# A projection kernel's first loads: single row tiles of x between the first k-tiles of w, cast and turned one row at a time, with fewer dummy matmuls

## The chip, the cores and the metric

One core of one Trainium2 chip. The metric is device time in microseconds (us) of one execution, as the median of several runs. A profile of one execution covers a span some 1.8 us shorter than the time of the same run.

## The reference

```python
def reference(x, w_qkv):              # x [16, 512, 768] f32, w_qkv [768, 2304] f32
    qkv = np.matmul(x, w_qkv)
    q, k, v = qkv[..., :768], qkv[..., 768:1536], qkv[..., 1536:]
    return np.stack([q, k, v], axis=0).astype(np.float32)
```

It is one product of 8192 x 768 by 768 x 2304, written out as three pieces.

## The kernel before

The x rows are handled in 32 pairs of row tiles (2 x 128 rows). From the fourth pair on, each pair is multiplied by a scheme that saves products, with sums of blocks of x made by GpSimd and sums of blocks of w made by VectorE. The first three pairs are multiplied plainly while those sums are being made. The change touches only the start of this plain part. "Turning" is a transpose on TensorE into PSUM, copied out by VectorE (first half) and ScalarE (second half). `busy(n)` issues n dummy 128x512 matmuls of zeros, to keep TensorE active until there is work.

```python
def load_rows(p):                      # two row tiles, 768 KB in one load
    xin[p] = xin_pool.tile([P, 2, K], fp32, name="xin")
    rows = x_flat[p * 2 * P:(p + 1) * 2 * P, :]
    nc.sync.dma_start(xin[p][:], rows.rearrange("(r m) k -> m r k", m=P))
...
load_rows(0)
...
load_rows(1)
load_blocks(0, 0, 1)                   # first w block: six k-tiles of 256 KB
load_w(st_rem[:], 0, KT, R_OFF, REM)   # 256 remainder columns of w
load_rows(2)
load_blocks(0, 1)                      # second w block, 768 KB halves
...
singles = [((0, ), (0, 1)), ((1, ), (0, 1)), ((0, 1), (2, 3))]     # (k-tiles, row tiles)
singles += [((j, ), range(4)) for j in range(2, KT)]
...
busy(11)
cast_rows(0)
turn_rows(0)
busy(4)
cast_rows(1)
cast_k(0)
cast_k(1)
turn_rows(1)
for j in range(2, KT):
    cast_k(j)
... # cast of the remainder columns
block(0, 0, b1[0], singles, nothing)   # four row tiles, first w block
rem(0)
rem(1)                                 # the same rows, remainder columns
cast_rows(2, False)
turn_rows(2, False)
block(0, 0, b1[0], halves((4, 5)), nothing)
... # second w block: the marker of this study
```

Of the kernel before, what the change touches and what calls it, by code (L numbers as in the profile page):

```python
# [10 lines left out]
def kernel(  # L11
# [20 lines left out]
    nc = tc.nc  # L32
    P = 128
# [3 lines left out]
    K = H  # L37
    N3 = w_qkv.shape[1]
    KT = K // P
    KH = KT // 2  # L40
    KC = K // 4
    NP = M // (2 * P)
    CB = 512
    REM = N3 - 4 * CB
    Q_OFF = (0, 2 * CB + REM)
    R_OFF = 2 * CB
    fp32 = mybir.dt.float32
    f32r = mybir.dt.float32r
    bf16 = mybir.dt.bfloat16
    ident = mybir.ActivationFunctionType.Identity  # L50
# [3 lines left out]
    x_flat = x.rearrange("b t h -> (b t) h")  # L54
# [5 lines left out]
    tq_pool = ctx.enter_context(tc.tile_pool(name="tq", bufs=2))  # L60
# [4 lines left out]
    xin_pool = ctx.enter_context(tc.tile_pool(name="xin", bufs=3))  # L65
    xf_pool = ctx.enter_context(tc.tile_pool(name="xf", bufs=2))
    xb_pool = ctx.enter_context(tc.tile_pool(name="xb", bufs=4))
    s_pool = ctx.enter_context(tc.tile_pool(name="s", bufs=2))
    ps_pool = ctx.enter_context(tc.tile_pool(name="ps", bufs=8, space=bass.MemoryType.PSUM))

    w_rem = w_pool.tile([P, KT, REM], bf16, name="w_rem")

    b1 = [w_pool.tile([P, KT, CB], bf16, name=f"b1_{q}") for q in range(2)]
# [7 lines left out]
    def load_w(dst, j0, nj, off, cols):  # L81
        rows = w_qkv.rearrange("(p j) n -> p j n", j=KT)
        nc.sync.dma_start(dst, rows[:, j0:j0 + nj, off:off + cols])

    stage = {}

    def load_blocks(q, c, nj=KH):
        if q == 0:
            t = tq_pool.tile([P, KT, CB], fp32, name="st0", tag="tq")
            for j in range(0, KT, nj):  # L90
                load_w(t[:, j:j + nj], j, nj, Q_OFF[q] + c * CB, CB)
            stage[q, 0, c], stage[q, 1, c] = t[:, :KH, :], t[:, KH:, :]
        else:
            for h in range(2):
                t = st_pool.tile([P, KH, CB], fp32, name="st1", tag="st")
                load_w(t[:], h * KH, KH, Q_OFF[q] + c * CB, CB)
                stage[q, h, c] = t[:]
# [11 lines left out]
    xin, xf, xb, sr = {}, {}, {}, {}  # L109
# [19 lines left out]



    def load_rows(p):
        xin[p] = xin_pool.tile([P, 2, K], fp32, name="xin")
        rows = x_flat[p * 2 * P:(p + 1) * 2 * P, :]
        nc.sync.dma_start(xin[p][:], rows.rearrange("(r m) k -> m r k", m=P))

    def copy_halves(dst, src, two):

        nc.vector.tensor_copy(out=dst[0], in_=src[0])  # L139
        if two:  # L140
            nc.scalar.activation(dst[1], src[1], ident)  # L141
        else:
            nc.vector.tensor_copy(out=dst[1], in_=src[1])

    xc = {}

    def cast_rows(p, two=True):
        src = xin.pop(p)
        xc[p] = s_pool.tile([P, 2, K], bf16, name="xc", tag="s")
        for r in range(2):  # L150
            halves = (slice(0, K // 2), slice(K // 2, K))
            copy_halves([xc[p][:, r, n] for n in halves], [src[:, r, n] for n in halves], two)

    def turn_rows(p, two=True):
        c = xc.pop(p)
        xb[p] = xb_pool.tile([P, KT, 2 * P], bf16, name="xb")
        for r in range(2):
            cols = c[:, r, :].rearrange("m (p j) -> m j p", j=KT)
            ps = ps_pool.tile([P, KT, P], bf16, name="ps")
            for j in range(KT):  # L160
                nc.tensor.transpose(ps[:, j, :], cols[:, j, :], eye)  # L161
            ks = (slice(0, KH), slice(KH, KT))
            copy_halves(
                [xb[p][:, n, r * P:(r + 1) * P] for n in ks], [ps[:, n, :] for n in ks], two
            )

    def round_x(p):
        xb[p] = xb_pool.tile([P, KT, 2 * P], bf16, name="xb")
# [42 lines left out]
    def bank():  # L211
        return ps_pool.tile([P, CB], fp32, name="ps")
# [29 lines left out]
    def rows_of(s, p, lo, hi):  # L242
        return out_flat[s, p * 2 * P:(p + 1) * 2 * P, lo:hi].rearrange("(r m) n -> m r n", m=P)

    def store_quad(u):
        if u.q == 0:
            nc.sync.dma_start(rows_of(0, u.p, 0, H), u.o[:, :, :H])
            nc.sync.dma_start(rows_of(1, u.p, 0, 2 * CB - H), u.o[:, :, H:])
        else:
            part = 2 * H - Q_OFF[1]  # L250
            nc.sync.dma_start(rows_of(1, u.p, H - part, H), u.o[:, :, :part])
            nc.sync.dma_start(rows_of(2, u.p, 0, H), u.o[:, :, part:])

    def rem_row(p, r, ps):
        for j in range(KT):
            nc.tensor.matmul(  # L256
                ps, xb[p][:, j, r * P:(r + 1) * P], w_rem[:, j, :],
                start=(j == 0), stop=(j == KT - 1), skip_group_check=True,
            )

    def rem(p):
        ps = ps_pool.tile([P, 2, REM], fp32, name="ps")
        for r in range(2):
            rem_row(p, r, ps[:, r, :])
        o = or_pool.tile([P, 2, REM], fp32, name="orem")
        nc.scalar.activation(o[:], ps[:], ident)  # L266
        nc.sync.dma_start(rows_of(1, p, R_OFF - H, R_OFF - H + REM), o[:])
# [70 lines left out]
    NS = 3  # L338
    zero = w_pool.tile([P, CB], bf16, name="zero")
    nc.vector.memset(zero[:], 0.0)  # L340
    load_rows(0)
    tiny = w_pool.tile([P, 1], fp32, name="tiny")
    nc.scalar.activation(tiny[:], zero[:, :1], ident)

    eye = w_pool.tile([P, 240], bf16, name="eye")[:, :P]
    make_identity(nc, eye)
    load_rows(1)
    load_blocks(0, 0, 1)
    st_rem = o_pool.tile([P, KT, REM], fp32, name="str", tag="o")
    load_w(st_rem[:], 0, KT, R_OFF, REM)  # L350
    load_rows(2)
    load_blocks(0, 1)
    load_blocks(1, 0)
    load_blocks(1, 1)
    load_x(3, nc.sync)
# [2 lines left out]
    def busy(n):  # L358

        ps = bank()  # L360
        for _ in range(n):
            nc.tensor.matmul(ps[:], zero[:, :P], zero[:], start=True, stop=True)  # L362
# [9 lines left out]
    def block(q, c, w, groups, cast_next):  # L372


        ps = {}
        for js, tiles in groups:
            for n in tiles:
                p, r = divmod(n, 2)
                if n not in ps:
                    ps[n] = bank()  # L380
                for j in js:
                    nc.tensor.matmul(  # L382
                        ps[n][:], xb[p][:, j, r * P:(r + 1) * P], w[:, j, :],
                        start=(j == 0), stop=(j == KT - 1), skip_group_check=True,
                    )
                if KT - 1 not in js:
                    continue
                if r == 0:
                    cast_next(p)
                u = quads[q][p]  # L390
                nc.scalar.activation(u.o[:, r, c * CB:(c + 1) * CB], ps[n][:], ident)
                if c == 1 and r == 1:
                    store_quad(u)

    def halves(tiles):
        return [(range(h * KH, (h + 1) * KH), tiles) for h in range(2)]


    singles = [((0, ), (0, 1)), ((1, ), (0, 1)), ((0, 1), (2, 3))]
    singles += [((j, ), range(4)) for j in range(2, KT)]  # L400

    act, dve = nc.scalar, nc.vector
    def cast_k(j):
        dve.tensor_copy(out=b1[0][:, j, :], in_=stage[0, j // KH, 0][:, j % KH, :])

    def cast_next(q, c, w):
        return lambda p: p < 2 and cast(q, p, c, w, act)

# [1 line left out]
        dve.tensor_copy(out=b1[0][:, j, :], in_=stage[0, j // KH, 0][:, j % KH, :])  # L410

    nothing = lambda p: None
    busy(11)
    cast_rows(0)
    turn_rows(0)
    busy(4)
    cast_rows(1)
    cast_k(0)
    cast_k(1)
    turn_rows(1)  # L420
    for j in range(2, KT):
        cast_k(j)
    act.activation(w_rem[:, KH:], st_rem[:, KH:], ident)
    dve.tensor_copy(out=w_rem[:, :KH], in_=st_rem[:, :KH])
    bt0 = bt_pool.tile([P, KT, CB], bf16, name="bt")
    bt1 = bt_pool.tile([P, KT, CB], bf16, name="bt")

    block(0, 0, b1[0], singles, nothing)
    rem(0)
    rem(1)  # L430
    cast_rows(2, False)
    turn_rows(2, False)
    block(0, 0, b1[0], halves((4, 5)), nothing)
    for h in range(2):
        cast(0, h, 1, bt0, dve)
    for n in range(1, 5):
        sum_w(0, n)
    dve.tensor_copy(out=b22[0][:], in_=stage[0, 1, 1])
    block(0, 1, bt0, halves(range(6)), cast_next(1, 0, b1[1]))
    load_x(4, nc.sync)  # L440
    block(1, 0, b1[1], halves(range(6)), cast_next(1, 1, bt1))
# [56 lines left out]
```

## Time and profile before

| | kernel before |
|---|---|
| time, median of the first three runs | 362.76 us (362.67 to 362.77) |
| span of the profiled run (which took 363.17 us) | 361.4 us |
| TensorE (PE) busy | 353.3 us, 98% |
| dummy matmuls | 15 |
| second w block starts at | 20.54 us |

The prediction below shows the lines. A timeline line reads: start, length, engine, line of the kernel, operation, tiles, count, and in brackets how long the engine was idle before and what released it. Merged matmul lines include the drain of the last one, so a length is a little over count times pace.

### The profile page before, as it was taken

Reading aid. Unit: us, or ns where it says so; the run is one execution under the profiler, and the core shown is the slowest. Engines: PE = TensorE matmul, PEld = TensorE weight load, DVE = VectorE, ACT = ScalarE, POOL = GpSimd, SP = SyncE. Lnnn points to the kernel's source line nnn. Section 1 sums busy time; section 2 is a strip of 40 time slices with the busy share of each in tenths; the row PEclk is TensorE's granted clock in tenths of the full one; section 3 lists DMA queues with packets and bytes.
Section 4 is the critical chain, followed back from the end, with each engine's and each line's share of the span. In section 5 each row is a group of like instructions: output and inputs, shape, how many; then the busy total and the mean of one; then the engine's idle time right before and its main releaser. Section 6 shows DMA issues by size and latency. Waiting matters only on the chain.

```text
span 361.4 us, 5220 instructions
## 1 busy us (share of the span) xinstructions
PE 353.3 (98%) x1765; PEld 250.8 (69%) x1797; DVE 222.7 (62%) x239; ACT 182.5 (51%) x304; POOL 174.4 (48%) x180
## 2 busy tenths in 40 slices
PE   8999999999999999999999999999999999999994
PEld 3644577777777777777777777777777777777763
DVE  3489546666566765566675565676556676556642
ACT  4547555455454545454545444445545454545452
POOL 0000970566664445664445665444666444566410
PEclk9999999999999999999999999999999999999999
DMA  7999969799899989999999999898999998989766
GB/s 294 381 383 338 348 227 345 271 354 304 279 322 298 296 275 296 282 313 314 284 278 295 282 306 316 284 276 291 295 285 317 295 296 276 297 279 331 267 251 242
DMA packets 80617, 108.08 MB, mean 299 GB/s; under 512 B 4816, under 2 KB 60368, under 8 KB 80592
## 3 DMA queue, kind: packets, MB, share of 16 engines
q1 hardware_dynamic: 65184, 96.35, 82.3%
q10 hardware_dynamic: 15408, 11.41, 9.9%
q8 instruction: 14, 0.23, 0.3%
q14 instruction: 11, 0.09, 0.1%
HBM read 32.24 MB, written 75.50 MB: 298 GB/s over the span
## 4 chain that ended last, share of the span: by engine, by line
PE 96%; ACT 1%; issue 1%; ACTq 0%; DVE 0%
PE ps L206 75%; PE ps L256 11%; PE ps L382 9%; PE ps L362 1%; PE ps L161 1%; ACT o L237 0%; ACTq L297 0%; ACT xb L141 0%; ACT orem L311 0%; DVE xb L139 0%; ACT xc L141 0%; ACTq L313 0%; DVE zero L340 0%; ACTq L311 0%
## 5 line engine op out<-in xcount | busy, mean ns | idle before, releaser
L206 PE MATMUL ps<-t,s 128*128 128x512 f32 x696 | 173.8, 398 | 0.0
L206 PEld LDWEIGHTS ps<-t,s 128*128 128x128 f32 x696 | 130.7, 188 | 29.8
L169 POOL CAST xb<-xf 128x1536 bf16<-128x1536 f32 x29 | 46.4, 1601 | 167.7 <-DVE xf L124 167.7
L234 DVE TENSOR_TENSOR o<-o,ps 128x512 f32<-128x512 f32 x58 | 39.9, 688 | 87.6 <-ACT o L233 87.6
L124 DVE STREAM_TRANSPOSE xf<-xin 128x1536 f32<-128x1536 f32 x29 | 85.7, 2956 | 9.7 <-DMA xin<-in_x_dram 7.1
L206 PE MATMUL ps<-b,xb 128*128 128x512 bf16 x320 | 82.4, 380 | 1.5
L233 ACT ACTIVATE o<-ps 128x512 f32<-128x512 f32 x58 | 34.7, 598 | 44.3 <-PE ps L206 44.3
L206 PEld LDWEIGHTS <-xb 128*128 128x128 bf16 x348 | 31.7, 98 | 35.6 <-issue 7.6
L227 ACT ACTIVATE o<-ps 128x512 f32<-128x512 f32 x58 | 34.8, 600 | 40.0 <-PE ps L206 37.3
L240 DVE TENSOR_TENSOR o<-o,ps 128x512 f32<-128x512 f32 x58 | 39.9, 688 | 21.4 <-PE ps L206 20.2
L206 PE MATMUL ps<-b,s 128*128 128x512 f32 x174 | 48.7, 389 | 0.0
L256 PE MATMUL ps<-w_rem,xb 128*128 128x256 bf16 x384 | 47.2, 273 | 0.0
L237 ACT ACTIVATE o<-ps 128x512 f32<-128x512 f32 x58 | 34.7, 598 | 24.1 <-PE ps L206 21.3
L220 ACT ACTIVATE o<-ps 128x512 f32<-128x512 f32 x58 | 34.6, 597 | 23.8 <-DVE o L240 20.7
L256 PEld LDWEIGHTS <-xb 128*128 128x128 bf16 x384 | 37.4, 98 | 11.2 <-issue 0.5
L224 DVE TENSOR_TENSOR o<-o,ps 128x512 f32<-128x512 f32 x58 | 36.5, 673 | 3.4 <-PE ps L206 2.1
L206 PEld LDWEIGHTS ps<-b,s 128*128 128x128 f32 x174 | 32.7, 188 | 6.8
L178 POOL TENSOR_TENSOR s<-s,xf 128x384 fp32r<-128x384 f32 x29 | 29.5, 1016 | 2.3
L266 ACT ACTIVATE orem<-ps 128x512 f32<-128x512 f32 x31 | 18.6, 598 | 22.7 <-PE ps L256 21.4
L179 POOL TENSOR_TENSOR s<-xf 128x384 fp32r<-128x384 f32 x29 | 29.5, 1017 | 0.0
L181 POOL TENSOR_TENSOR s<-xf,s 128x384 fp32r<-128x384 f32 x29 | 29.4, 1015 | 0.0
L177 POOL TENSOR_TENSOR s<-xf 128x384 fp32r<-128x384 f32 x29 | 29.3, 1012 | 0.0
(36 smaller groups left out, 127.2 us busy)
## 6 DMA issues: line engine op xcount, KB each, us to landing
out_dram<-o SPq DMA_DIRECT2D x62, 768.0 KB, 5.1
out_dram<-o SPq DMA_DIRECT2D x65, 256.0 KB, 4.6
xin<-in_x_dram SPq DMA_DIRECT2D x62, 192.0 KB, 6.7
xin<-in_x_dram ACTq DMA_DIRECT2D x54, 192.0 KB, 4.5
out_dram<-orem SPq DMA_DIRECT2D x31, 256.0 KB, 5.5
st<-in_w_qkv_dram SPq DMA_DIRECT2D x6, 768.0 KB, 14.1
xin<-in_x_dram SPq DMA_DIRECT2D x3, 768.0 KB, 5.8
st<-in_w_qkv_dram SPq DMA_DIRECT2D x6, 256.0 KB, 6.3
```

The costliest lines, as they stand in the source:

```text
L124: nc.vector.transpose(t[:].rearrange("p j (g b) -> p g j b", b=G), xin.pop(p)[:].rearrange("p g (a j) -> p g j a", a=G),)
L169: nc.gpsimd.tensor_copy(out=xb[p][:], in_=xf[p][:])
L206: nc.tensor.matmul(ps[:], lhs[j], rhs[j], start=(start and j == 0), stop=(j == KH - 1), skip_group_check=True,)
L220: nc.scalar.activation(c11, u.x[:], ident)
L224: nc.vector.tensor_tensor(c11, c11, u.z[:], op=add)
L227: nc.scalar.activation(c12, u.x[:], ident)
L233: nc.scalar.activation(c22, u.x[:], ident)
L234: nc.vector.tensor_tensor(c22, c22, u.y[:], op=add)
L237: nc.scalar.activation(c21, u.x[:], ident)
L240: nc.vector.tensor_tensor(c12, c12, u.y[:], op=add)
L256: nc.tensor.matmul(ps, xb[p][:, j, r * P:(r + 1) * P], w_rem[:, j, :], start=(j == 0), stop=(j == KT - 1), skip_group_check=True,)
L382: nc.tensor.matmul(ps[n][:], xb[p][:, j, r * P:(r + 1) * P], w[:, j, :], start=(j == 0), stop=(j == KT - 1), skip_group_check=True,)
```

## The change

The intent: the first row tile is usable one transfer sooner if it is not tied to the second, and a fourth row tile is not needed until the first three have been multiplied by five k-tiles. So rows 0, 1 and 2 come singly, then k-tiles 0 to 4, row 3, k-tile 5; casts and turns are done row by row, and fewer dummies should be needed. The remainder's two halves, of which ScalarE cast one before, are both cast by VectorE.

```diff
-    load_rows(0)
+    load_row(0, 0)                     # 384 KB each
 ...
-    load_rows(1)
-    load_blocks(0, 0, 1)
+    load_row(0, 1)
+    load_row(1, 0)
+    for j in range(KT - 1):
+        load_k(j)
+    load_row(1, 1)
+    load_k(KT - 1)
-    load_w(st_rem[:], 0, KT, R_OFF, REM)
-    load_rows(2)
+    for h in range(2):
+        load_w(st_rem[:, h * KH:(h + 1) * KH], h * KH, KH, R_OFF, REM)
+    for r in range(2):
+        load_row(2, r)
 ...
-    busy(11)
-    cast_rows(0)
-    turn_rows(0)
-    busy(4)
-    cast_rows(1)
-    cast_k(0)
-    cast_k(1)
-    turn_rows(1)
-    for j in range(2, KT):
+    busy(8)
+    cast_row(0, 0)
+    cast_row(0, 1)
+    turn_row(0, 0)
+    busy(1)
+    cast_row(1, 0)
+    turn_row(0, 1)
+    cast_k(0)
+    turn_row(1, 0)
+    for j in range(1, KT - 1):
         cast_k(j)
 ... (helpers by row; the fourth row's cast and turn stand between k-tiles 4 and 5)
-    block(0, 0, b1[0], singles, nothing)
-    rem(0)
-    rem(1)
-    cast_rows(2, False)
-    turn_rows(2, False)
-    block(0, 0, b1[0], halves((4, 5)), nothing)
+    block(0, 0, b1[0],
+        [((j, ), range(3)) for j in range(KT - 1)]
+        + [fourth_row, ((KT - 1, ), range(3)), (range(KT), (3, ))], nothing)
+    for p in range(2):
+        rem(p)
+        cast_row(2, p, False)
+        turn_row(2, p, False)
+    block(0, 0, b1[0], [(range(KT), (4, )), (range(KT), (5, ))], nothing)
```

More of the change, by code (lines that the diff above doesn't have):

```diff
@@ L128, in transpose, with load_row @@
         xf[p] = t
-    def load_rows(p):
-        xin[p] = xin_pool.tile([P, 2, K], fp32, name="xin")
-        rows = x_flat[p * 2 * P:(p + 1) * 2 * P, :]
-        nc.sync.dma_start(xin[p][:], rows.rearrange("(r m) k -> m r k", m=P))
+    def load_row(p, r):
+        if r == 0:
+            xin[p] = xin_pool.tile([P, 2, K], fp32, name="xin")
+        row = (2 * p + r) * P
+        nc.sync.dma_start(xin[p][:, r, :], x_flat[row:row + P, :])
     def copy_halves(dst, src, two):
@@ L145, with cast_row, turn_row @@
     xc = {}
-    def cast_rows(p, two=True):
-        src = xin.pop(p)
-        xc[p] = s_pool.tile([P, 2, K], bf16, name="xc", tag="s")
-        for r in range(2):
-            halves = (slice(0, K // 2), slice(K // 2, K))
-            copy_halves([xc[p][:, r, n] for n in halves], [src[:, r, n] for n in halves], two)
-    def turn_rows(p, two=True):
-        c = xc.pop(p)
-        xb[p] = xb_pool.tile([P, KT, 2 * P], bf16, name="xb")
-        for r in range(2):
-            cols = c[:, r, :].rearrange("m (p j) -> m j p", j=KT)
-            ps = ps_pool.tile([P, KT, P], bf16, name="ps")
-            for j in range(KT):
-                nc.tensor.transpose(ps[:, j, :], cols[:, j, :], eye)
-            ks = (slice(0, KH), slice(KH, KT))
-            copy_halves(
-                [xb[p][:, n, r * P:(r + 1) * P] for n in ks], [ps[:, n, :] for n in ks], two
-            )
+    def cast_row(p, r, two=True):
+        if r == 0:
+            xc[p] = s_pool.tile([P, 2, K], bf16, name="xc", tag="s")
+        halves = (slice(0, K // 2), slice(K // 2, K))
+        copy_halves([xc[p][:, r, n] for n in halves], [xin[p][:, r, n] for n in halves], two)
+    def turn_row(p, r, two=True):
+        if r == 0:
+            xb[p] = xb_pool.tile([P, KT, 2 * P], bf16, name="xb")
+        cols = xc[p][:, r, :].rearrange("m (p j) -> m j p", j=KT)
+        ps = ps_pool.tile([P, KT, P], bf16, name="ps")
+        for j in range(KT):
+            nc.tensor.transpose(ps[:, j, :], cols[:, j, :], eye)
+        ks = (slice(0, KH), slice(KH, KT))
+        copy_halves(
+            [xb[p][:, n, r * P:(r + 1) * P] for n in ks], [ps[:, n, :] for n in ks], two
+        )
     def round_x(p):
@@ L346, with load_k @@
     make_identity(nc, eye)
-    load_rows(1)
-    load_blocks(0, 0, 1)
-    st_rem = o_pool.tile([P, KT, REM], fp32, name="str", tag="o")
-    load_w(st_rem[:], 0, KT, R_OFF, REM)
-    load_rows(2)
-    load_blocks(0, 1)
+    st_0 = tq_pool.tile([P, KT, CB], fp32, name="st0", tag="tq")
+    stage[0, 0, 0], stage[0, 1, 0] = st_0[:, :KH, :], st_0[:, KH:, :]
+    def load_k(j):
+        load_w(st_0[:, j:j + 1], j, 1, Q_OFF[0], CB)
+    load_row(0, 1)
[4 more added lines that the diff above has]
+    load_k(KT - 1)
+    st_rem = o_pool.tile([P, KT, REM], fp32, name="str", tag="o")
+    for h in range(2):
+        load_w(st_rem[:, h * KH:(h + 1) * KH], h * KH, KH, R_OFF, REM)
+    for r in range(2):
+        load_row(2, r)
+    load_blocks(0, 1, KH)
     load_blocks(1, 0)
@@ L375, in block @@
         ps = {}
-        for js, tiles in groups:
+        for group in groups:
+            if callable(group):
+                group()
+                continue
+            js, tiles = group
             for n in tiles:
@@ L396, in halves @@
         return [(range(h * KH, (h + 1) * KH), tiles) for h in range(2)]
-    singles = [((0, ), (0, 1)), ((1, ), (0, 1)), ((0, 1), (2, 3))]
-    singles += [((j, ), range(4)) for j in range(2, KT)]
     act, dve = nc.scalar, nc.vector
-    def cast_k(j):
-        dve.tensor_copy(out=b1[0][:, j, :], in_=stage[0, j // KH, 0][:, j % KH, :])
     def cast_next(q, c, w):
@@ L412, with fourth_row @@
     nothing = lambda p: None
-    busy(11)
-    cast_rows(0)
-    turn_rows(0)
-    busy(4)
-    cast_rows(1)
+    busy(8)
[5 more added lines that the diff above has]
+    turn_row(0, 1)
     cast_k(0)
-    cast_k(1)
-    turn_rows(1)
-    for j in range(2, KT):
+    turn_row(1, 0)
+    for j in range(1, KT - 1):
         cast_k(j)
-    act.activation(w_rem[:, KH:], st_rem[:, KH:], ident)
-    dve.tensor_copy(out=w_rem[:, :KH], in_=st_rem[:, :KH])
+    def fourth_row():
+        cast_row(1, 1)
+        cast_k(KT - 1)
+        turn_row(1, 1)
+        for h in range(2):
+            ks = slice(h * KH, (h + 1) * KH)
+            dve.tensor_copy(out=w_rem[:, ks], in_=st_rem[:, ks])
     bt0 = bt_pool.tile([P, KT, CB], bf16, name="bt")
     bt1 = bt_pool.tile([P, KT, CB], bf16, name="bt")
-    block(0, 0, b1[0], singles, nothing)
-    rem(0)
-    rem(1)
-    cast_rows(2, False)
-    turn_rows(2, False)
-    block(0, 0, b1[0], halves((4, 5)), nothing)
+    block(
+        0, 0, b1[0],
+        [((j, ), range(3)) for j in range(KT - 1)]
+        + [fourth_row, ((KT - 1, ), range(3)), (range(KT), (3, ))],
+        nothing,
+    )
+    for p in range(2):
[3 more added lines that the diff above has]
+    block(0, 0, b1[0], [(range(KT), (4, )), (range(KT), (5, ))], nothing)
     for h in range(2):
```

## The prediction

> **What bounds the kernel now.** I read the page first: busy shares, then the chain that ended last. Then I asked for PE's waits over the whole run, and for the first 22 us in order of time, because the change touches nothing later.
>
> ```profile
> PE 353.3 (98%) x1765; PEld 250.8 (69%) x1797; DVE 222.7 (62%) x239; ACT 182.5 (51%) x304; POOL 174.4 (48%) x180
> ...
> PE 96%; ACT 1%; issue 1%; ACTq 0%; DVE 0%
> PE ps L206 75%; PE ps L256 11%; PE ps L382 9%; PE ps L362 1%; PE ps L161 1%; ACT o L237 0%; ACTq L297 0%; ACT xb L141 0%; ACT orem L311 0%; DVE xb L139 0%; ACT xc L141 0%; ACTq L313 0%; DVE zero L340 0%; ACTq L311 0%
> ```
>
> PE is the chain almost everywhere. Line 362 is the group of dummy matmuls that bridges the wait for the first rows; it is on the chain but computes nothing. PE's waits, all of them in the run:
>
> ```profile
> PE ps L362 <- DVE zero L340: 1.2, 1, 1.2
> PE ps L161 <- ACT xc L141: 0.6, 1, 0.6
> ```
>
> Both are before 8.5 us. After that PE waits for nothing the profile resolves, so what counts is how early PE can start useful work and never stop. The start in order of time (start, length, engine, line):
>
> ```profile
> 0.74 0.95 SPq L135 DMA_DIRECT2D xin<-in_x_dram  x2
> 1.19 4.88 PE L362 MATMUL ps<-zero 128*128 128x512 bf16 x11 [1.19 <-DVE zero L340]
> 5.08 0.94 ACT L141 ACTIVATE xc<-xin 128x384 bf16<-128x384 f32 x2 [2.85 <-DMA xin<-in_x_dram]
> 5.86 1.11 PE L161 MATMUL ps<-eye,xc 128*128 128x128 bf16 x12
> 6.81 1.03 PE L362 MATMUL ps<-zero 128*128 128x512 bf16 x4
> 7.07 0.87 ACT L141 ACTIVATE xb<-ps 128x384 bf16<-128x384 bf16 x2 [1.05 <-DVE xb L139]
> 8.40 0.95 PE L161 MATMUL ps<-eye,xc 128*128 128x128 bf16 x12 [0.57 <-ACT xc L141]
> 9.19 5.34 PE L382 MATMUL ps<-b,xb 128*128 128x512 bf16 x23
> 11.11 0.43 DVE L410 CAST b<-st 128x512 bf16<-128x512 f32 x1 [0.26 <-DMA st<-in_w_qkv_dram]
> 13.37 0.56 DVE L424 CAST w_rem<-str 128x768 bf16<-128x768 f32 x1 [1.83 <-DMA str<-in_w_qkv_dram]
> 14.37 2.78 PE L256 MATMUL ps<-w_rem,xb 128*128 128x256 bf16 x24
> 15.43 0.36 DVE L139 CAST xc<-xin 128x384 bf16<-128x384 f32 x1 [1.50 <-DMA xin<-in_x_dram]
> 16.99 0.83 PE L161 MATMUL ps<-eye,xc 128*128 128x128 bf16 x12
> 17.94 2.76 PE L382 MATMUL ps<-b,xb 128*128 128x512 bf16 x11
> 20.54 7.93 PE L382 MATMUL ps<-bt,xb 128*128 128x512 bf16 x36
> ```
>
> The reader should see three things. The first 768 KB of x are usable at 5.08 us, and PE fills the time with dummies. From 6.97 to 8.40 PE again does nothing useful: four dummies and a gap, until the second pair of rows is loaded and cast. From 8.40 to 20.54 PE is full: 12 transposes, 24 matmuls, 24 remainder matmuls, 12 transposes, 12 matmuls. I take 20.54, where the second w block starts, as the marker: everything after it is the same program in both kernels.
>
> **What the Trainium skill says.** "TensorE: Matmul & The Clock Gate", section "What's actually happening": the array runs at half clock until about 3.4 us of sustained activity have been seen. The trace agrees: the dummies start 0.43 us apart, the real 128x512 matmuls run at 0.216 (24 from 9.19 to 14.37). The granted-clock row of the page does not show it (9 tenths in every slice). "DMA: Bandwidth & Descriptors", section "Latency and other measured facts", speaks of a fixed cost of about 2 us for a DMA. Here the first load is issued at 0.74 and usable at 5.08, 4.34 us; its 786 thousand bytes at the measured 400 GB/s take 1.97, so 2.4 us are fixed, which agrees. "PSUM — Partial Sum Buffer", section "PSUM bank collisions raise a hardware error", says that two engines must not touch one bank at once. The trace agrees in form: ACT's copy out of the transposed bank (7.07) starts only when DVE's 0.36 us copy of it, from 6.67, is over.
>
> **The change part by part.**
>
> Loads. Bytes are the same, the order is not: x row tiles 0, 1, 2 (393 thousand bytes each, 0.98 us at 400 GB/s), k-tiles 0 to 4 of w (262 thousand, 0.66 us each), row tile 3, k-tile 5, the remainder block in two halves, rows 4 and 5. The stream starts at 0.74 + 2.4 = 3.1 us in landing times. Rows land at about 4.1, 5.1 and 6.1; k-tiles at 6.7, 7.4, 8.0, 8.6, 9.3; row 3 at 10.3; k-tile 5 at 11.1 as before (same bytes ahead of it; DVE had waited for it at 11.11). The remainder's halves land at 12.3 and 13.37, rows 4 and 5 at 14.4 and 15.43, the later ones again as before. Five more issues at about 0.45 us of SP's queue each cost nothing: the built program lets eight loads be outstanding, and at any time these hold over 2 MB, 5 us of stream.
>
> Dummies. 11 + 4 become 8 + 1. Eight at 0.43 us end at 1.19 + 3.42 = 4.61; the first row's casts end at 4.1 + 0.52 (ACT's half) = 4.6. So useful work starts at 4.65 instead of 5.86, 1.2 us earlier.
>
> From there I walk PE, each start being the later of PE free and data ready. Durations are from the rows above and from single instructions of the same groups: DVE cast 0.35, ACT cast 0.52, DVE copy out 0.36, ACT copy out 0.45, k-tile cast 0.43, six transposes 0.64 cold and 0.4 warm.
> Row 0 turned 4.65 to 5.3, dummy to 5.6, row 1 turned 5.6 to 6.1. Row 2 is cast by 6.65 (ACT, after its copy for row 0), but its turn ends about 7.1. k-tile 0 is cast at 7.14 (DVE: two other steps first).
> Blocks of 3 matmuls, 0.65 each: k0 7.15 to 7.8, k1 8.0 to 8.65, k2 to 9.3, k3 to 9.95, k4 to 10.6. Row 3 (landed 10.3, cast by 10.8) turns 10.85 to 11.25. k5 is cast 11.1 to 11.53: 11.55 to 12.2. Tile 3 by itself, 6 matmuls: 12.2 to 13.5.
> Remainder: three matmuls of 0.109 to 13.83, then a wait for the second half (13.37 + 0.56 = 13.93), nine more to 14.95.
> Row 4 is cast 14.4 to 15.03, turned 15.1 to 15.5; remainder of rows 2 and 3 15.5 to 16.8; row 5 cast by 16.85, turned to 17.3. Two tiles of 6 matmuls (1.3 each): 17.3 to 19.9.
> The second block starts at 19.9 instead of 20.54: 0.64 us earlier.
>
> So of the 1.2 us at the start and the 1.43 at 6.97, some 2 us come back as small gaps: DMA pace between k-tiles, row 3, the remainder's second half. A check from the other side: the second half of the remainder cannot be used before 13.95, and 21 remainder matmuls (2.29), 12 transposes (0.8) and 12 matmuls (2.6) follow it, 5.7 us, so 19.65 is the floor while the loads keep their times.
>
> What follows must not eat the gain. The second block's first half is cast by DVE from about 18.0 (its copies end there), 0.95, done 18.9: before 19.9. Its second half is usable at 20.87 + 0.96 = 21.83; PE needs it 18 matmuls (3.9) after 19.9, at 23.8. The next block's first half is cast by ACT until 24.3, needed at 27.7. The POOL sums for the first group of Strassen-like products end at 45.8, needed at 48.2 (48.88 less the gain). Each has 2 us or more of room. At the end PE is again the chain up to 353 us, so the shift reaches the end. Predicted: 362.76 - 0.64 = 362.1.
>
> **The rivals.**
> First, cold clock. The dummies now stop sooner and small gaps stand among transposes from 5.3 to 7.1, so the gate may open late. For: in the kernel before it opened near 6.6 after unbroken work. Against: the share of work in that window is still about nine tenths. If it stays cold to 9.9, the block up to there does 6 matmuls instead of 12 and PE is about 1.2 us late at 10.6; part of that fits in the waits after it, and the marker comes at about 20.2. Time 362.4; with a longer cold stretch 363.
> Second, the loads set the end and the gain is nothing. For: the remainder's cast was at 13.37 and its use at 14.37, close behind; the DMA share is full in this window. If the smaller loads land some 0.5 us later than their bytes say, the remainder and rows 4, 5 push PE back to where it was: 362.6 to 362.8.
> Third, more gain. The gaps I count for row 5 and the remainder may be hidden, or DMA may begin with the small row sooner than I think; the floor of 19.65 gives 361.9, and if remainder halves land earlier than the whole did, 361.5.
> Fourth, the earlier stores and loads of the next stage collide. DMA engines are full from 16 to 40 us, but PE needs nothing from them sooner than 2 us after their old landings, so I give it little.
>
> **Range and chances.** The centre is the walk, 362.1. The cold clock and late loads bound it above, the floor with a little more below: 361.6 to 362.7 for 8 in 10. Two per cent are 7.3 us; all time before useful work is 5.9 us, plus 1.4 later, so a faster verdict is out of reach, and a slower one would need the start to double. Faster 0.005, within 2% 0.99, slower 0.005.
>
> **What would show it.** First transposes near 4.65 (step one), first real matmul near 7.15, k-tile groups spaced 0.65 by the casts, remainder from 13.5, second block near 19.9, and the steady stage shifted by the same amount with its 10.7 us period unchanged. The prediction is wrong if matmuls of the first block take 0.43 us, if the first row is not usable before 4.6, or if PE shows waits after 20 us that the kernel before did not have.

## More of the kernel before

One view is added here, because the answer turned on it. It has one line for a stretch of time: the stretch, its length, busy time of PE, PEld (weight loads), DVE (VectorE), ACT (ScalarE) and POOL (GpSimd), the granted share of the TensorE clock, the busy share of the DMA engines, and GB/s. Kernel before, 4 to 6 us:

```profile
4.00:6.00 2.00, 2.00 (x7) 0.72 (x6) 0.63 (x2) 0.92 (x2) 0.00 (x0) 1.00 1.02 412
```

The loads stream at 412 GB/s here.

## The result and the profile after

Measured: 364.21 us median of six runs (363.08 to 364.34), against 362.74 of the kernel before (six runs, 362.67 to 363.44). The ratio is 1.0031, with a 95% interval of 1.0017 to 1.0046. Ratios here are the mean time of one kernel's runs over that of the other's of the same rounds, so not quite the ratio of the medians. The forecast was 0.7 us faster; it came out about 1.1 to 1.5 us slower. By the 2% rule both are "same", but the sign is clear.

PE's waits in the changed kernel (total, times, longest), all of them:

```profile
PE ps L160 <- ACT xc L142: 1.6, 2, 1.4
PE ps L374 <- DVE zero L339: 1.2, 1, 1.2
```

The wait for a cast row (line 160 is the turn) grew from 0.6 to 1.6 us. The start in order of time:

```profile
0.74 1.34 SPq L136 DMA_DIRECT2D xin<-in_x_dram  x3
1.18 3.52 PE L374 MATMUL ps<-zero 128*128 128x512 bf16 x8 [1.18 <-DVE zero L339]
3.75 0.52 ACT L142 ACTIVATE xc<-xin 128x384 bf16<-128x384 f32 x1 [1.53 <-DMA xin<-in_x_dram]
4.54 0.50 PE L160 MATMUL ps<-eye,xc 128*128 128x128 bf16 x6
4.87 0.52 ACT L142 ACTIVATE xc<-xin 128x384 bf16<-128x384 f32 x1 [0.60 <-DMA xin<-in_x_dram]
...
5.45 0.54 PE L160 MATMUL ps<-eye,xc 128*128 128x128 bf16 x6 [0.20 <-ACT xc L142]
...
6.81 0.52 ACT L142 ACTIVATE xc<-xin 128x384 bf16<-128x384 f32 x1 [0.78 <-DMA xin<-in_x_dram]
7.39 0.54 PE L160 MATMUL ps<-eye,xc 128*128 128x128 bf16 x6 [1.40 <-ACT xc L142]
7.99 5.03 PE L399 MATMUL ps<-b,xb 128*128 128x512 bf16 x15
11.82 0.43 DVE L420 CAST b<-st 128x512 bf16<-128x512 f32 x1 [0.34 <-DMA st<-in_w_qkv_dram]
12.86 0.50 PE L160 MATMUL ps<-eye,xc 128*128 128x128 bf16 x6
21.16 7.93 PE L399 MATMUL ps<-bt,xb 128*128 128x512 bf16 x36
```

The first two rows are early: usable at 3.75 and 4.87, both before the 5.08 of the pair. The third row comes at 6.81, not at 6.1. Then 15 matmuls take 5.03 us, where the walk had 3.45 us (7.15 to 10.6). The second block starts at 21.16 instead of 20.54. From there on the two kernels take the same: 23.31 us each for the three other plain blocks, and for the rest 317.4 us (changed) and 317.6 us (before). All of the profiled difference arises before 21 us. The two profiled runs took 363.17 us (before) and 363.70 us (changed), so this pair of traces shows only 0.5 us of the difference.

Two things show in the view by stretches, for the changed kernel:

```profile
4.00:6.00 2.00, 1.79 (x15) 0.89 (x13) 0.74 (x3) 1.26 (x3) 0.00 (x0) 1.00 0.97 320
```

```profile
4.51:7.91 3.40, 1.81 (x20) 1.19 (x19) 1.65 (x5) 1.98 (x4) 0.00 (x0) 1.00 0.96 336
7.93:11.32 3.39, 3.33 (x8) 1.13 (x8) 2.18 (x7) 0.72 (x3) 0.00 (x0) 0.50 1.05 393
11.34:14.74 3.40, 3.40 (x22) 1.70 (x21) 1.86 (x5) 1.26 (x4) 0.00 (x0) 1.00 1.07 382
```

First, the loads fell from 412 to 320 GB/s between 4 and 6 us, although the DMA engines count as busy. Second, the granted clock was 0.50 from 7.92 to 11.33. In the 3.4 us just before, PE had been busy for 1.81. The trace's own clock records, which no line here shows, give the edges as 4.506 (full), 7.919 (half), 11.332 (full): 3.413 us apart each time. The time in front of the first record counts as full clock in this view, though the dummies there ran 0.43 us apart; so the page's clock row does not show a late opening.

Two causes were thus on the table. "Clock": with fewer dummies and a longer pause, the clock gate (closed, TensorE runs at half clock) closes again or opens late. "Loads": small loads at the start make the stream itself slower.

### The profile page after: what moved, and what is told of

Read it like the earlier page. It is cut to its first block, busy times and chain, and to the rows that moved or that the text cites. A ratio compares the mean times of both kernels' runs of the same rounds, so it can differ in the third digit from the quotient of the medians.

```text
span 361.9 us, 5243 instructions
## 1 busy us (share of the span) xinstructions
PE 354.7 (98%) x1791; PEld 250.1 (69%) x1791; DVE 225.5 (62%) x240; ACT 182.3 (50%) x303; POOL 173.8 (48%) x180
## 4 chain that ended last, share of the span: by engine, by line
PE 96%; DMA 1%; ACT 1%; ACTq 0%; SPq 0%; issue 0%; DVE 0%
PE ps L205 75%; PE ps L255 11%; PE ps L399 9%; DMA st<-in_w_qkv_dram 1%; SPq L136 0%; ACT o L236 0%; ACTq L296 0%; PE ps L160 0%; ACT orem L310 0%; DVE b L420 0%; ACTq L312 0%; ACTq L310 0%
## 5 line engine op out<-in xcount | busy, mean ns | idle before, releaser
L168 POOL CAST xb<-xf 128x1536 bf16<-128x1536 f32 x29 | 43.8, 1512 | 168.9 <-DVE xf L124 134.5
L205 PE MATMUL ps<-b,xb 128*128 128x512 bf16 x348 | 84.9, 380 | 0.0
L176 POOL TENSOR_TENSOR s<-xf 128x384 fp32r<-128x384 f32 x29 | 30.8, 1064 | 0.0
L178 POOL TENSOR_TENSOR s<-xf 128x384 fp32r<-128x384 f32 x29 | 29.5, 1016 | 0.0
```

Of the source, the lines that this page charges most:

```text
L168: nc.gpsimd.tensor_copy(out=xb[p][:], in_=xf[p][:])
L205: nc.tensor.matmul(ps[:], lhs[j], rhs[j], start=(start and j == 0), stop=(j == KH - 1), skip_group_check=True,)
```

## The experiments

Kernels of one call ran on the same chip, each call on another one, and shared the runs of the kernel before: 362.77 us median in the first call (11 runs), 362.99 in the second (9), 362.83 in the third (11). Its runs are not all alike either: they fall near 362.7 and near 363.3, so a tenth of a per cent needs the intervals. All results were correct.

### again: the changed kernel once more

No edit.

> The changed kernel unaltered, for more runs and a second trace. Theory clock (the gate closes again in the gap before the third row's turn): times scatter between about 363.0 and 364.4, and a trace with a long time has a stretch at half clock after 4.5 us or opens late. Theory loads (the small first loads land late): the third row tile again lands near 6.8 us instead of 6.1, in every trace alike, and the times do not scatter.

Measured: 363.70 us (362.97 to 364.69, 6 runs), ratio 1.0024 (1.0010 to 1.0038). The times scatter by 1.7 us, as theory clock says, though the loads differ between the two traces too. The second trace shows the gate closing too, in another place:

```profile
3.93:7.33 3.40, 1.61 (x15) 0.82 (x13) 0.83 (x4) 1.38 (x4) 0.00 (x0) 1.00 0.85 288
7.35:10.75 3.40, 2.95 (x12) 1.48 (x13) 2.53 (x8) 1.38 (x3) 0.00 (x0) 0.50 1.04 404
```

Half clock from 7.34 to 10.75, again 3.41 us, after a stretch of the same length in which PE was busy for 1.61. The third row was cast at 7.22 us, later still; so theory loads holds in both traces of this kernel, but not its claim that times would not scatter.

The record also holds the mean granted clock of every run. A half-clock stretch of 3.41 us takes 0.005 off it, and no trace without such a stretch after the opening is below 0.997. Nine of the changed kernel's twelve runs have 0.992 to 0.995, so the gate very probably closed in each of them. The two fastest, 363.08 and 362.97 us, have 1.000. One of 364.20 us has 0.999; why it was slow is not shown.

### fill5: dummies into the gap

```diff
     turn_row(0, 1)
+    busy(5)
     cast_k(0)
```

> The changed kernel with five dummy matmuls more, between the second row's turn and the third row's, where PE waited 1.4 us. Theory clock: no half-clock stretch after opening, the first block's matmuls at 0.22 us, spread under 0.5 us, time about 362.2 to 362.8, so 1.4 us or more faster than the changed kernel. Theory loads: the third row still comes at 6.8 us, and the time stays at 363.5 or more.

Measured: 363.20 us (362.91 to 363.64, 5 runs), ratio 1.0009 (0.9997 to 1.0021), 0.5 us under the unaltered kernel.

```profile
3.40:6.80 3.40, 3.40 (x18) 1.82 (x17) 1.29 (x5) 1.85 (x4) 0.00 (x0) 1.00 0.93 303
6.81:10.20 3.39, 3.37 (x20) 1.54 (x19) 2.25 (x7) 1.18 (x3) 0.00 (x0) 1.00 1.04 392
```

The gate opened at 6.81 and stayed open; the first block's 15 matmuls took 3.70 us instead of 5.03, and the spread fell to 0.7 us. All five runs have a mean clock of 0.997 or more. That is theory clock. But the loads still ran at 303 GB/s in the first of these stretches, the third row was cast at 6.49, and the second block began at 20.68. The gain was a third of what theory clock alone had promised, and neither theory's time was met. The trace shows both causes at work. The difference of the times alone is less sure, as the intervals of the two kernels overlap (1.0009, 0.9997 to 1.0021, against 1.0024, 1.0010 to 1.0038).

### fewer_dummies: the dummies alone, in the kernel before

```diff
-    busy(11)
+    busy(8)
     cast_rows(0)
     turn_rows(0)
-    busy(4)
+    busy(1)
```

> The kernel before with its loads and order of work untouched, but 8 + 1 dummies instead of 11 + 4. Theory clock: PE now pauses 1 us before the first turn and nearly 1.5 us before the second, so the gate opens late or closes again: slower by 0.5 to 1.5 us, with scatter. Theory loads: 362.7 as before, since dummies compute nothing and the loads are the same.

Measured: 364.25 us (363.94 to 365.67, 6 runs), ratio 1.0041 (1.0027 to 1.0055).

```profile
3.44:6.84 3.40, 2.52 (x16) 1.34 (x15) 0.93 (x3) 0.94 (x2) 0.00 (x0) 1.00 1.02 409
6.85:10.25 3.40, 2.44 (x18) 1.58 (x17) 2.25 (x8) 2.25 (x5) 0.00 (x0) 1.00 1.06 393
10.26:13.66 3.40, 3.40 (x10) 1.20 (x9) 1.79 (x6) 0.83 (x3) 0.00 (x0) 1.00 1.08 368
```

The loads run at full rate (409 GB/s). The 1.00 in the clock column is the quirk named above: the first record of an open gate in this trace is at 13.67 us. From 9.80 to there nine wide matmuls were done, 0.43 us each. In the two stretches ahead PE was busy for 2.52 and 2.44 of 3.40, and the gate did not open; it opened right after the first stretch that was full. With nothing changed but six dummies that compute nothing, the kernel lost 1.5 us by the medians. This trace is of the slowest run, 365.67 us, and its second block began at 23.07. The five others (363.94 to 364.55 us) have a mean clock of 0.992 to 0.995, against 0.997 here, so in them the gate very probably opened sooner and closed again; no trace shows where.

### split_rows: single-row loads alone, in the kernel before

```diff
-        nc.sync.dma_start(xin[p][:], rows.rearrange("(r m) k -> m r k", m=P))
+        for r in range(2):
+            nc.sync.dma_start(xin[p][:, r, :], rows[r * P:(r + 1) * P, :])
```

> The kernel before with each pair load of x rows split into two single-row loads, all else the same. Theory loads: the stream falls behind, the sixth k-tile is cast near 11.8 us instead of 11.1, the time rises by 0.4 us or more. Theory clock: the same as before within 0.2 us, as PE's first work and dummies are where they were.

Measured: 364.09 us (363.72 to 364.42, 5 runs), ratio 1.0027 (1.0014 to 1.0040).

```profile
4.00:6.00 2.00, 1.76 (x13) 0.92 (x12) 0.72 (x3) 0.76 (x2) 0.00 (x0) 1.00 0.78 250
```

The rate falls to 250 GB/s, and the last k-tile is cast at 13.01 us instead of 11.11. Theory clock's "same within 0.2 us" failed; its gate was open from 4.46 us in this trace, and with a mean clock of 0.999 or more it did not close in any of the five runs. So the form of the loads costs about a microsecond by itself (1.0 us by the ratio, 1.3 by the medians).

### first_split, second_split, col_split: what about the loads?

The first splits only the first pair's load, the second only the second pair's. The third splits both pairs by columns, so that each load still holds two row tiles.

```diff
+        if p == 0:                     # first_split; p == 1 in second_split
+            for r in range(2):
+                nc.sync.dma_start(xin[p][:, r, :], rows[r * P:(r + 1) * P, :])
+        else:
             nc.sync.dma_start(xin[p][:], rows.rearrange("(r m) k -> m r k", m=P))
```

```diff
-        nc.sync.dma_start(xin[p][:], rows.rearrange("(r m) k -> m r k", m=P))
+        both = rows.rearrange("(r m) k -> m r k", m=P)
+        for h in (slice(0, K // 2), slice(K // 2, K)):
+            nc.sync.dma_start(xin[p][:, :, h], both[:, :, h])
```

> The kernel before with the first pair load alone split into two single-row loads; the second stays whole. Theory starve (small loads at the very start leave the engines short of queued work): nearly all of the delay of the full split, sixth k-tile cast near 12.5 us, +0.8 us or more. Theory row pattern (each single-row load is slow by itself): half of it. Rival (only the loads after 4 us matter): nothing.

> The kernel before with the second pair load alone split. Theory starve: little, under 0.3 us, since the first large load has built up a backlog. Theory row pattern: about half of the full split's 1 us. Its sixth k-tile is cast near 11.1 us for the first, near 11.8 for the second.

> The kernel before with each pair load split by columns, two loads of 384 KB that each still hold both row tiles, in rows of 1536 bytes. Theory small size (number and size of the loads): the stream dips as in the split by rows and the time rises by about 1 us. Theory row pattern (a single row tile's 128 pieces of 3 KB): no dip, 362.8 as before.

| run | time, us | ratio (95%) | GB/s, 4 to 6 us | last k-tile cast at |
|---|---|---|---|---|
| first_split | 364.57 (4 runs) | 1.0049 (1.0035 to 1.0063) | 195 | 12.93 |
| second_split | 362.98 (4 runs) | 0.9999 (0.9983 to 1.0014) | 365 | 11.69 |
| col_split | 363.92 (4 runs) | 1.0027 (1.0014 to 1.0041) | 283 | 12.87 |

```profile
4.00:6.00 2.00, 2.00 (x7) 0.75 (x6) 0.36 (x1) 0.65 (x2) 0.00 (x0) 1.00 0.82 195
```

This line is first_split's. Splitting the first load alone costs all that splitting both did (1.0049 against 1.0027). It was run on another chip. Splitting the second delays the k-tiles by 0.6 us but not the run, as PE had that much room. Its k-tile came at 11.69, where theory row pattern had 11.8 and theory starve 11.1; its time is what theory starve said. The split by columns dips as well, which speaks against the pattern of a single row tile; but its pieces are shorter too, 1536 bytes, so by itself it does not exclude that pattern. And in first_split what comes late is not a small load: the two small ones are cast at 3.60 and 4.95; it is the unchanged 768 KB load behind them, cast at 8.87 instead of 7.28. The loads behind a short start are late.

The same trace limits what can be said of the gate:

```profile
6.32:9.72 3.40, 1.73 (x19) 1.01 (x18) 1.48 (x5) 1.72 (x4) 0.00 (x0) 1.00 1.03 365
```

PE was busy for 1.73 us here, less than the 1.81 us after which the gate closed in the changed kernel, yet the clock, recorded as full from 6.31 on, stayed full, and the 24 matmuls after it took 5.37 us. So the busy time of a stretch does not decide alone. Turns were 1.56 of the 1.81 us and 1.06 of the 1.61 us in the two stretches that closed the gate, and 0.87 of the 1.73 us here; whether that is the reason was not tested.

### pair_first and pair_again: both causes mended

```diff
-    load_row(0, 0)
+    xin[0] = xin_pool.tile([P, 2, K], fp32, name="xin")
+    nc.sync.dma_start(xin[0][:], x_flat[:2 * P, :].rearrange("(r m) k -> m r k", m=P))
 ...
-    load_row(0, 1)
     load_row(1, 0)
 ...
-    busy(8)
+    busy(11)
 ...
     turn_row(0, 1)
+    busy(3)
     cast_k(0)
```

> The changed kernel with its first two rows loaded as one pair, 11 dummies in front and 3 more after the second row's turn, so that the stream starts with a large load and PE is never idle for long. Theories clock and loads together: the third row lands near 6.1 to 6.3 us, gate open by 8 us, k-tiles at 0.65 us, second block near 20.0 us and 362.2 to 362.6 us, below the kernel before. If the third row and the k-tiles still dip, theory starve is wrong and the time is 363 or more.

> The version with the first two rows as one pair and its dummies, once more, to see whether it beats the kernel before: 362.4 to 362.9, below the kernel before of the same rounds by 0.1 to 0.5 us, second block near 20.3 us.

Measured: 362.68 us (362.44 to 362.85, 5 runs), ratio 0.9992 (0.9979 to 1.0004); the second time 362.51 us (362.33 to 362.70, 5 runs), ratio 0.9989 (0.9977 to 1.0001). From the first trace, the stretch from 4 to 6 us:

```profile
4.00:6.00 2.00, 1.82 (x12) 0.78 (x10) 0.63 (x2) 0.94 (x2) 0.00 (x0) 1.00 1.00 385
```

and PE in order of time:

```profile
5.60 0.54 PE L160 MATMUL ps<-eye,xc 128*128 128x128 bf16 x6 [0.18 <-ACT xc L142]
...
7.90 3.70 PE L399 MATMUL ps<-b,xb 128*128 128x512 bf16 x15
...
20.32 2.97 PE L399 MATMUL ps<-bt,xb 128*128 128x512 bf16 x13
```

The rate is back at 385 GB/s, and the first block runs at the pace of its k-tiles (15 matmuls in 3.70 us). The first row is turned a microsecond later than in the changed kernel, yet the second block starts 0.84 us sooner. The first time lies just above what was expected, the second within it. It is below the changed kernel beyond doubt (the intervals do not touch). Against the kernel before, it was about 0.1% faster in both. Each interval alone just includes 1, so "probably a little faster" is all that is shown.

### first_split_act and fill5_act: the second row from another queue

```diff
-                nc.sync.dma_start(xin[p][:, r, :], rows[r * P:(r + 1) * P, :])
+                (nc.sync, nc.scalar)[r].dma_start(xin[p][:, r, :], rows[r * P:(r + 1) * P, :])
```

fill5_act does the same to row 1 of fill5, and issues it directly behind row 0 in the program.

> The kernel before with the first pair split as in the run of that name, but the second row's load issued from ACT's queue, so that the second pair's load is issued as early as in the kernel before (second in its queue). Theory lead (the third load in one queue is not ready to stream when two small ones are done at 4 us): no dip, second pair landed by 7.1 us, 362.8 to 363.2. Theory small (two small loads ahead upset the stream however they are issued): second pair near 8.8 us, 364 or more.

> The changed kernel with five more dummies and its second row's load issued from ACT's queue. Theory lead: third row landed near 6.0 instead of 6.5, k-tiles earlier by as much, 362.3 to 362.7. Theory small: third row at 6.5 or later, 363.2 as with the dummies alone.

Measured, first_split_act: 363.01 us (362.51 to 363.22, 4 runs), ratio 1.0000 (0.9987 to 1.0013).

```profile
4.00:6.00 2.00, 2.00 (x7) 0.75 (x6) 0.63 (x2) 0.94 (x2) 0.00 (x0) 1.00 1.02 409
```

The same two small loads, the same bytes, but 409 GB/s instead of 195, and all of the 1.6 us is gone. Theory small falls: two small loads ahead do not upset the stream however they are issued. This fits theory lead: the big load behind them is now issued at 1.18 us, second in its queue, and not at 1.65, third. The two rows then land together (cast at 4.79).

Measured, fill5_act: 362.84 us (362.60 to 364.33, 6 runs), ratio 1.0004 (0.9989 to 1.0019). From 4 to 6 us it moved 383 GB/s against 303 in fill5, and the last k-tile was cast at 11.43 instead of 11.91. The median was 0.36 us below fill5's, but the intervals overlap. It was run on another chip. One run at 364.33 has no trace; it is left unexplained. The median of all six is just above what theory lead had forecast. This run leans towards theory lead without settling it.

## Why the prediction was wrong

**Right.** The mechanism of the gain was there. The first turn was expected at 4.65 and came at 4.54; the second at 5.6, and came at 5.45 (4.26 and 5.81 in the second trace). The first is partly luck: it started when the dummies ended, while its row was usable at 3.75 and not at the 4.1 of the walk. Nothing later ate the shift: from the second block on, both kernels take the same time. And the conclusion that 2% are out of reach held.

**Wrong, first term: the landings.** The step was "The stream starts at 0.74 + 2.4 = 3.1 us in landing times", with every later load placed by its bytes at 400 GB/s. That rate came from a stream that began with 768 KB loads. The stream with single rows ran at 320 GB/s from 4 to 6 us (240 in the second trace), so row 2 was cast at 6.81 instead of 6.1 and everything after it came some 0.7 us late: k-tile 5 at 11.82 instead of 11.1. My second rival had this, as "if the smaller loads land some 0.5 us later than their bytes say", but I gave it no mechanism. I also argued, in the walk, that over 2 MB outstanding meant the "five more issues" (by the diff, four) "cost nothing"; first_split and first_split_act show that the order and the queue of issue did matter. The cost can be read from fill5, which has these loads and an open gate: its second block starts at 20.68, against 19.9 in the walk, 0.8 us. The k-tiles bear this out: in fill5, pair_first and pair_again the last one was cast at 11.91, 11.54 and 11.34 us, 0.8, 0.4 and 0.2 us after the walk's 11.1, and the second block began at 20.68, 20.32 and 20.11, 0.8, 0.4 and 0.2 us after the walk's 19.9.

**Wrong, second term: the clock.** The first rival's "the share of work in that window is still about nine tenths" was mis-sized. The late third row made the pause 1.40 us, and in the 3.4 us that counted PE was busy for 1.81, or 53%. The gate closed for 3.41 us, and the first block's 15 matmuls took 5.03 us instead of 3.45. The prediction had named this sign of its being wrong: "if matmuls of the first block take 0.43 us". What the half-clock stretch cost in the end: 21.16 less 20.68 in the two traces, 0.5 us, and 0.5 us between the medians of the unaltered kernel and fill5 (363.70 and 363.20). The two terms sum to 1.3 us: 19.9 + 0.8 + 0.5 = 21.2, the measured start of the second block; as each is a difference of starts, this sum is no check of the split. In the second trace the split is another one: the last k-tile was cast at 12.26, 1.2 us after the walk's 11.1, and the second block began at 21.13, also 1.2 us after the walk. By this measure the half-clock stretch added next to nothing there, because the loads were later still. The median of all runs was worse than the first trace; at which point the gate closed in those runs is not recorded, only their mean clock.

**The link between the two.** I treated the rivals as separate. They were chained: the late load made the pause, and the pause closed the gate (with the pause filled, in fill5, it stayed open). The dummies that the change took away are what had covered both in the kernel before. Taken away alone they cost 1.5 us (fewer_dummies); in the traced run, the slowest, the gate opened only at 13.67.

**What stays open.** Why the loads behind a short start stall is not settled. The stall came with the short loads in one queue and ahead of the others (first_split), hardly with them second (second_split), and not with them in two queues (first_split_act). In first_split_act two things changed together: the big load was issued 0.47 us earlier, and it stood second in its queue. Which of them matters was not told apart. Nor is it settled what exactly closes the gate, since 1.81 us of work in 3.4 closed it and 1.73 did not.

## What to carry to other kernels

Dummy matmuls are not free to remove: here they held the clock open through the pauses. Before cutting them, add up PE's busy time over each stretch of 3.4 us, and take a half-empty stretch as a warning, not as a rule. A landing time worked out from a measured rate holds only while the loads ahead of it keep their size and queue; keep the first load of a stream large, or issue the small ones from two queues. When two rivals in a prediction touch the same moment, ask whether one causes the other.

## What the Trainium skill lacked or had wrong

- "TensorE: Matmul & The Clock Gate", sections "What's actually happening" and "HAM oscillation — how this bites in real kernels": these sections name idle gaps of over about 3.4 us as what closes the gate (the section "A second HAM failure mode: psum-queue depth-cycling" lets short idle times close it too, without a figure). Here the longest pause was 1.40 us, and the gate closed; in col_split a pause of 1.98 us left it open. The runs show how busy PE was in a window of 3.4 us and what the gate did: 1.81 and 1.61 us busy, closed; 1.73 (first_split), 2.00 (col_split) and 2.83 (kernel before, 6.44 to 9.84), stayed open; 2.52 and 2.44, did not open; 2.73 (the run again, 0.52 to 3.92), 2.93 (fill5_act, 3.71 to 7.11) and 3.40, opened. For closing, busy time alone thus gives no threshold. The window length itself agrees: 3.413 us between the edges. The page warns that clock events can be unreliable, but not that the time before the first opening has no record, so that a view of granted clock reads 1.00 while matmuls run 0.43 us apart (fewer_dummies, up to 13.67 us).
- "DMA: Bandwidth & Descriptors", section "Issuing engines are not separate DMA queues": it says that issuing from several engines only saves the sequencer's time. At the start of the stream this can be worth more than the time saved: one 384 KB load moved to ACT's queue brought the next issue forward by 0.47 us, raised the rate from 4 to 6 us from 195 to 409 GB/s and took 1.6 us off the run. Whether the earlier issue or the place in the queue did it was not told apart, so the page is not shown to be wrong.
- The same page, section "Measured (HBM→SBUF, 128 partitions, SWDGE, issued from GpSimd)", ties the rate to the size of a load. Here 256 KB loads in mid-stream ran at about 400 GB/s in the kernel before; no page says that small loads at the very start slow the loads behind them (first_split: the unchanged 768 KB load cast at 8.87 us instead of 7.28).
